# Tying interleaved VectorE work to the weight stream, and wider value matmuls, in a two-layer hybrid decoder trunk

## The chip, the cores and the metric

The kernel runs on one core of one Trainium2 chip. The metric is device time in microseconds (us) for one execution, and the figure for the kernel before is the median of three runs. A profile of one further execution gives the rows below. TensorE (PE) multiplies, VectorE (DVE) and ScalarE (ACT) do elementwise work and read PSUM, GpSimd (POOL) does elementwise work on SBUF, and SyncE (SP) issues all DMA loads and stores.

## The reference

Two layers work on x of shape 512 x 1024 (one batch). Per layer, in float32:

```
mod = silu(c) @ w_ada + b_ada                  # 6 x 1024: sh1, sc1, g1, sh2, sc2, g2
h = x * (1 + sc1) + sh1
p = h @ w_in                                   # q,k,v,g of retention; q,f,v,g of HGRN2; conv a,b; gates
u_a = retention(...); u_b = hgrn2(...); u_c = silu(LN(dwconv31(ca * sigmoid(cb))))
y = sum over 3 branches of sigmoid(gate_i) * (u_i @ w_branch[i])
x = LN(ALPHA * x + g1 * (y @ w_out)) * ln1_g + ln1_b
h = x * (1 + sc2) + sh2
f = (silu(a) * v) @ w_down,  a, v = split(dwconv3(h @ w_up))        # d_ff 2816
x = LN(ALPHA * x + g2 * f) * ln2_g + ln2_b
```

Retention and HGRN2 have four heads of 128 each, the convolution has 512 channels and 31 taps.

## The kernel before

**Layout.** Activations lie feature-major: a tile is 128 features by 512 tokens. Each float32 operand of a large matmul is kept as two float32r parts, a high part `hi` and the rest `lo`, and `mm3` issues three matmuls for a product (hi x hi, hi x lo, lo x hi; lines 249 to 251). Weights come in chunks of 128 x 1024 (512 KB). The function `w_plan` writes their order out by hand for each layer.

**Weight stream.** `prefetch` takes a chunk through three steps: a DMA into `raw` (line 215, 4 buffers of the tag "raw"), a copy on ScalarE to `hi` (line 216) and a subtraction on VectorE for `lo` (line 217; 4 buffers each). `chunk(kind, ahead)` makes sure that the wanted chunk and `ahead` further ones have been prefetched and hands out the first; the usual `ahead` is LA = 2. Most projections (`proj`) use one chunk for 24 matmuls of 512 columns.

**Stages of a layer.** An input projection for the convolution, then the mixing half in the order of MIX: values of HGRN2, HGRN2 heads 0 and 1, values of retention, HGRN2 head 2, retention 0, HGRN2 3, retention 1 to 3. Then come three branches in the order HGRN2, retention, convolution: for each pair of 128 output features two gate projections, one branch chunk, two products. A branch product is multiplied by the gate on VectorE (line 802), added to the sum on GpSimd (line 806), and after the last branch split into hi and lo (lines 229 and 231). Then the output projection with the first norm, the feed-forward half, and its norm.

**Interleaved work.** Work that doesn't follow the stream is written as generators. `heads` holds the recurrences of the heads, `fill` a queue of other work: rope tables, the 31 taps of the convolution in two pairs of tiles (60 instructions a pair, line 383), the norm of the convolution, conditioning columns, residuals. After every four contraction tiles the projections call `tick(us)`, which adds a credit of at most 3.0, advances up to three heads by a step each and then takes steps of the first fill entry while credit is left. Each step returns its cost in credit. Steps of heads are tied behind the last matmul with `tc.issue_after`; steps of `fill` are not. The tool that builds the program orders each engine's queue itself, by a simulated time at which an instruction becomes ready and by its place in the program; `issue_after(ins)` adds an edge to `ins` for instructions of its own engine, without a semaphore. `drain(fill)` at the end of the mixing half finishes what is left.

**Conditioning.** `ada_col(l, i)` loads one 128 x 1024 chunk of w_ada (line 191) into a buffer of the same tag "raw" as the weights, multiplies and sums it against silu(c) (line 195) and adds the bias (line 196). Layer 0's first 16 columns are done in the start stage, 24 in the mixing half (as `rest(aux)` behind the convolution's norm), 8 in the feed-forward half, and the next layer's first 16 in the down projection. `affine` then computes eight gains and eight shifts one column at a time (lines 661 and 662) and two scaled copies (lines 664 and 666).

**Values.** `proj_tok` computes values token-major: h is the stationary operand, the weight chunk moves. Two groups of 256 columns are computed with two chunks each, a chunk holding 4 contraction tiles x 256 columns.

Of the kernel before, what the change touches and what calls it, by code (L numbers as in the profile page):

```python
# [20 lines left out]
P = 128  # L21
# [8 lines left out]
NB = 47  # L30
NHL = 4
LA = 2
NRAW = 4
TK = 1.7
AUX = 99
# [18 lines left out]
def w_plan(l):  # L54
# [7 lines left out]
    def tok(seg):  # L62
        return [("tok", c, SEG[seg] + 256 * g) for g in range(2) for c in range(2)]
# [26 lines left out]
def trunk(ctx, tc, xT, cT, pos, ada, bada, wts, cols, lbl, rope_c, decay, hmask, outT):  # L90
# [73 lines left out]
    last = [None]  # L164

    def step(queue, g):
        try:
            if queue is heads:
                with tc.issue_after(last[0].ins):
                    return next(g)  # L170
            return next(g)
        except StopIteration:
            queue.remove(g)
            return 0.0
# [14 lines left out]
    def ada_col(l, i):  # L189
        raw = wp.tile([P, 1024], F32, tag="raw", name=nm("ar"), bufs=NRAW)  # L190
        nc.sync.dma_start(raw, ada[l, i])
        o = ADA[i]
        dst = modt[l][:, o:o + 1]
        yield 0.0
        stt(raw, raw, 1.0, cond, ALU.mult, ALU.mult, accum_out=dst)  # L195
        ts(dst, dst, bad[:, 48 * l + o:48 * l + o + 1], 1.0 if o // 8 in (1, 4) else 0.0, ALU.add, ALU.add)
        yield 1.3
# [5 lines left out]
    def prefetch(n=1):  # L203
        for _ in range(n):
# [8 lines left out]
            for o in range(0, 1024, n):  # L213
                s = slice(o, o + n)
                nc.sync.dma_start(raw[:, s], wts[l, i][:, s])
                act(hi[:, s], raw[:, s], AF.Copy)  # L216
                tt(lo[:, s], raw[:, s], hi.bitcast(F32)[:, s], ALU.subtract)  # L217
# [72 lines left out]
    def proj_tok(hs):  # L290
        for g in range(2):
            w = [chunk("tok", LA - 1), chunk("tok", LA - 1)]
            for tp in range(2):
                q = pm()
                for t2 in range(2):
                    tk = 2 * tp + t2
                    dst = q[:, 256 * t2:256 * (t2 + 1)]
                    for kt in range(KT):
                        mm3(dst, sl2(hs[kt], 128 * tk), sl2(w[kt // 4], 256 * (kt % 4), 256),
                            kt == 0, kt == KT - 1)  # L300
                    tick(1.5)
                yield g, tp, q
# [72 lines left out]
    def conv_taps(l, i0, us, out, aux):  # L375
# [5 lines left out]
        for d in range(1, CK):  # L381
# [4 lines left out]
            if d % AUX == 0 and aux:  # L386
                yield from aux.pop(0)

    def rest(aux):
        while aux:  # L390
            yield from aux.pop(0)
# [59 lines left out]
    def hgrn_head(l, h, q, f, ke, sg, v, out):  # L451
# [12 lines left out]
        while m <= 256:  # L464
# [44 lines left out]
            else:  # L509
                act(pf[:, 128:384], z[:, 0:256], AF.Copy)  # L510
                act(pf[:, 384:512], z[:, 256:384], AF.Copy)
                act(pg[:, 0:128], z[:, 384:512], AF.Copy)
            m, lev = 2 * m, lev + 1
            yield 1.2
# [143 lines left out]
    def affine(l, gname, bname, lm, sc, sh):  # L658
        for j in range(8):
            G, B = gbt[:, j:j + 1], gbt[:, 8 + j:9 + j]  # L660
            stt(G, col(l, gname, j), -0.5, mod(lm, sc, j), ALU.mult, ALU.mult)
            stt(B, col(l, bname, j), mod(lm, sc, j), mod(lm, sh, j), ALU.mult, ALU.add)
        o = CO[gname]
        ts(gbt[:, 16:24], colt[l][:, o:o + 8], -0.5 * ALPHA, None, ALU.mult)
        o = CO[bname]
        ts(gbt[:, 24:32], colt[l][:, o:o + 8], ALPHA, None, ALU.mult)
# [46 lines left out]
    for j in range(8):  # L713
        cs = [ada_col(0, 2 * j), ada_col(0, 2 * j + 1)]
        for g in cs:
            next(g)
        nc.sync.dma_start(X[j], xT[j])
        for g in cs:
            next(g)
# [8 lines left out]
    for l in range(L):  # L728
# [5 lines left out]
        aux = [ada_col(l, i) for i in range(16, 40)]  # L734
# [3 lines left out]
        for i in (0, 2):  # L738
# [5 lines left out]
            fill.append(conv_taps(l, i, us, acc, aux))  # L744
        fill.append(conv_norm(l, acc, u_c))
        fill.append(rest(aux))

        vg, vr = [big() for _ in range(4)], [big() for _ in range(4)]
        for what, h in MIX:
            if what == "g" and h < 0:  # L750
                for g, tp, q in proj_tok(hs):
                    for t2 in range(2):
                        act(vg[2 * tp + t2][:, 256 * g:256 * (g + 1)], q[:, 256 * t2:256 * (t2 + 1)], AF.Copy)
            elif h < 0:
                for g, tp, q in proj_tok(hs):
                    qv = q.rearrange("p (t h d) -> p t h d", h=2, d=128)
                    sm = bp.tile([P, 4], F32, tag="sm", name=nm("sm"), bufs=2)
                    nc.vector.tensor_reduce(sm, q.rearrange("p (a d) -> p a d", d=128),
                                            mybir.AxisListType.X, ALU.add)
                    for t2 in range(2):  # L760
                        stt(vr[2 * tp + t2][:, 256 * g:256 * (g + 1)].rearrange("p (h d) -> p h d", d=128),
                            sm[:, 2 * t2:2 * t2 + 2].unsqueeze(2).broadcast_to([P, 2, 128]), -1.0 / 128,
                            qv[:, t2], ALU.mult, ALU.add)
# [16 lines left out]
        for bi, b in enumerate(ORDER):  # L780
            us = (u_a, u_b, u_c)[b]
            for jp in range(4):
# [13 lines left out]
                for t in range(2):  # L796
# [6 lines left out]
                    if bi == 0:  # L803
                        ys[j] = sg[t]
                    else:
                        ptt(ys[j], ys[j], sg[t], ALU.add)  # L806
# [4 lines left out]
        affine(l, "ln1g", "ln1b", l, 4, 3)  # L811
# [28 lines left out]
        fill.extend(ada_col(l, i) for i in range(40, 48))  # L840
# [20 lines left out]
        if l == 0:  # L861
            fill.extend(ada_col(1, i) for i in range(16))
# [3 lines left out]
        for j in range(8):  # L866
            parts = HALVES if j == 7 else ((0, S),)
            if l == 0 and j == 7:
                drain(fill)
                affine(l, "ln2g", "ln2b", 1, 1, 0)  # L870
# [39 lines left out]
def _chunks(l, w_in, w_branch, w_out, w_up, w_down):  # L910
    out = np.empty((NW, 128, 1024), np.float32)
    down = w_down.reshape(FT, 128, 8, 128).transpose(2, 0, 1, 3).reshape(FT, 8, 128, 128)
    for i, p in enumerate(W_PLAN[l]):
# [10 lines left out]
        elif p[0] == "tok":  # L924
            out[i] = _ktile(w_in, 4 * p[1], 4, p[2], 256)
# [78 lines left out]
```

## Time and profile before

| | before |
|---|---|
| median of 3 runs | 1846.57 us (1845.42 to 1847.24) |
| the profiled execution | 1846.69 us |
| its span, first to last instruction | 1844.90 us |
| mean granted TensorE clock | 0.996 |
| PE busy | 1805.0 us, 98% |
| DVE busy | 1290.4 us, 70% |
| ACT busy | 751.4 us, 41% |
| POOL busy | 218.8 us, 12% |
| HBM read | 214.19 MB, 117 GB/s over the span |

Busy time is the union of an engine's instructions. Ends of matmuls are modelled and matmuls overlap, so a busy TensorE isn't one at its peak: the distance between the starts of matmuls says more than their durations. Times in the rows are us from the start of the span, durations in "mean" columns are ns. [...]

### The profile page before, as it was taken

What the parts mean: (1) busy time and instruction counts of PE and PEld (TensorE: products, weight loads), DVE (VectorE), ACT (ScalarE), POOL (GpSimd) and SP (SyncE); (2) the same over time, 40 slices, a digit from 0 to 9 for tenths busy, and PEclk for the clock granted to TensorE, in tenths of its full rate; (3) what the DMA queues carried; (4) which work ended last, traced back from release to release, by engine and by line L of the source; (5) the groups of instructions that cost most, each with busy time, mean ns of one, the idle gap of its engine ahead of it and who ended that gap; (6) DMA issues with size and microseconds to landing.
All of it is one profiled execution on the core that took longest, in us unless ns stands there. A gap on an engine that the chain in (4) does not pass through costs nothing.

```text
span 1844.9 us, 23510 instructions
## 1 busy us (share of the span) xinstructions
PE 1805.0 (98%) x9156; PEld 1520.0 (82%) x9156; DVE 1290.4 (70%) x2025; ACT 751.4 (41%) x1042; POOL 218.8 (12%) x187
## 2 busy tenths in 40 slices
PE   7999999999999999999999999999999999999997
PEld 5888877888788888888889987778787988888886
DVE  6995565978869756667489565993775896666344
ACT  3434344333337444432273344453523564444232
POOL 3111231042100000000000221320222000000001
PEclk9999999999999999999999999999999999999999
DMA  8512222226624422255223112222474244222221
GB/s 304 195 70 80 75 75 80 92 103 213 228 73 144 142 103 92 103 183 182 93 90 103 70 69 75 71 76 99 156 245 158 81 142 143 92 103 92 102 82 46
DMA packets 63614, 217.81 MB, mean 118 GB/s; under 512 B 7440, under 2 KB 9872, under 8 KB 63504
## 3 DMA queue, kind: packets, MB, share of 16 engines
q1 hardware_dynamic: 63504, 216.32, 34.2%
q8 instruction: 72, 1.18, 0.3%
q14 instruction: 38, 0.31, 0.1%
HBM read 214.19 MB, written 2.10 MB: 117 GB/s over the span
## 4 chain that ended last, share of the span: by engine, by line
PE 79%; DVE 11%; DMA 4%; ACT 2%; issue 2%; POOL 2%; SPq 0%; DVEq 0%; POOLq 0%; ACTq 0%
PE pm L249 24%; PE pm L251 24%; PE pm L250 24%; DMA ar<-ada 4%; DVE wl L217 2%; DVE ar L195 2%; PE ps L477 2%; DVE b L383 1%; POOL b L806 1%; ACT wh L216 1%; DVE x L655 1%; PE po L552 1%; PE ps L544 1%; DVE b L802 1%; PE ps L250 0%
## 5 line engine op out<-in xcount | busy, mean ns | idle before, releaser
L249 PE MATMUL pm<-h,wh 128*128 128x512 f32 (+1 forms) x1568 | 613.3, 391 | 13.3 <-ACT wh L216 11.6
L251 PE MATMUL pm<-h,wl 128*128 128x512 f32 (+1 forms) x1568 | 603.3, 385 | 0.2
L250 PE MATMUL pm<-h,wh 128*128 128x512 f32 (+1 forms) x1568 | 602.1, 384 | 0.0
L217 DVE TENSOR_TENSOR wl<-wr,wh 128x1024 fp32r<-128x1024 f32 (+1 forms) x301 | 376.8, 1254 | 251.6 <-ACT wh L216 250.5
L216 ACT ACTIVATE wh<-wr 128x1024 fp32r<-128x1024 f32 (+1 forms) x301 | 317.1, 1055 | 490.0 <-PE pm L250 385.2
L249 PEld LDWEIGHTS pm<-h,wh 128*128 128x128 f32 x1568 | 295.6, 188 | 72.0 <-ACT wh L216 11.6
L251 PEld LDWEIGHTS pm<-h,wl 128*128 128x128 f32 x1568 | 295.0, 188 | 61.3 <-DVE wl L217 3.4
L250 PEld LDWEIGHTS pm<-h,wh 128*128 128x128 f32 x1568 | 295.5, 188 | 58.8 <-issue 1.9
L249 PE MATMUL pm<-b,wh 128*128 128x512 f32 (+1 forms) x764 | 280.8, 368 | 6.1 <-ACT b L229 4.7
L250 PE MATMUL pm<-b,wh 128*128 128x512 f32 (+1 forms) x764 | 279.5, 366 | 0.4 <-DVE b L231 0.4
L251 PE MATMUL pm<-b,wl 128*128 128x512 f32 (+1 forms) x764 | 279.1, 365 | 0.0
L383 DVE SCALAR_TENSOR_TENSOR b<-b,cols,b 128x511 f32<-128x511 f32 (+14 forms) x240 | 171.9, 770 | 0.0
L249 PEld LDWEIGHTS pm<-b,wh 128*128 128x128 f32 x764 | 145.0, 190 | 30.5 <-ACT b L229 5.6
L250 PEld LDWEIGHTS pm<-b,wh 128*128 128x128 f32 x764 | 145.0, 190 | 24.5 <-DVE b L231 1.5
L195 DVE SCALAR_TENSOR_TENSOR ar<-ar,cond 128x1024 f32<-128x1024 f32 x96 | 123.5, 1293 | 58.9 <-DMA ar<-ada 58.8
L251 PEld LDWEIGHTS pm<-b,wl 128*128 128x128 f32 x764 | 144.9, 190 | 22.8
L229 ACT ACTIVATE b<-b 128x512 fp32r<-128x512 f32 x88 | 55.4, 630 | 230.7 <-DVE b L852 109.2
L231 DVE TENSOR_TENSOR b<-b,b 128x512 fp32r<-128x512 f32 x88 | 61.1, 694 | 51.9 <-ACT b L229 51.8
L490 POOL TENSOR_TENSOR b<-b,b 128x256 f32<-128x256 f32 x64 | 56.3, 879 | 324.9 <-PE ps L477 218.0
L806 POOL TENSOR_TENSOR b<-b,b 128x512 f32<-128x512 f32 x32 | 57.1, 1784 | 235.2 <-DVE b L802 222.8
L249 PE MATMUL pm<-wh,h 128*128 128x256 f32 x256 | 73.7, 289 | 0.0
L250 PE MATMUL pm<-wl,h 128*128 128x256 f32 x256 | 72.4, 283 | 0.6 <-DVE wl L217 0.6
(222 smaller groups left out, 1899.5 us busy)
## 6 DMA issues: line engine op xcount, KB each, us to landing
wr<-wts SPq DMA_DIRECT2D x299, 512.0 KB, 3.5
ar<-ada SPq DMA_DIRECT2D x96, 512.0 KB, 4.3
x<-xT SPq DMA_DIRECT2D x8, 256.0 KB, 5.8
b<-decay SPq DMA_DIRECT2D x8, 256.0 KB, 3.8
outT<-b SPq DMA_DIRECT2D x16, 128.0 KB, 1.8
b<-hmask SPq DMA_DIRECT2D x3, 256.0 KB, 5.9
cond<-cT SPq DMA_DIRECT2D x1, 512.0 KB, 4.7
wr<-wts SPq DMA_DIRECT2D x2, 256.0 KB, 6.7
```

Source lines behind the costliest of these rows:

```text
L195: stt(raw, raw, 1.0, cond, ALU.mult, ALU.mult, accum_out=dst)
L216: act(hi[:, s], raw[:, s], AF.Copy)
L217: tt(lo[:, s], raw[:, s], hi.bitcast(F32)[:, s], ALU.subtract)
L229: act(hi, src, AF.Copy)
L231: tt(lo, src, hi.bitcast(F32), ALU.subtract)
L249: mm(dst, a[0], b[0], start=first, stop=False)
L250: mm(dst, a[0], b[1], start=False, stop=False)
L251: last[0] = mm(dst, a[1], b[0], start=False, stop=end)
L383: stt(a[:, d:S], us[i][:, 0:S - d], col(l, "cw", 4 * (CK - 1 - d) + i0 + i), a[:, d:S], ALU.mult, ALU.add)
L477: mm(z[:, 64 * i:64 * (i + 1)], ke[:, sl], rhs, start=True, stop=True)
L490: ptt(kv[:, :, 0, :], kv[:, :, 0, :], fv[:, :, 1:2].broadcast_to([P, nb, m]), ALU.mult)
L806: ptt(ys[j], ys[j], sg[t], ALU.add)
```

## The change

- **Ties.** `step` puts every step, of heads and of fill, behind the last matmul and behind `wlast[1]`, the VectorE subtraction of the weight chunk prefetched last.
- **Conditioning.** `ada_cols` handles a list of columns: it issues the load of the next column before it sums the current one, has three buffers of its own, ties its loads behind the last weight load, and adds biases for eight columns in one instruction. It goes into `fill` as an ordinary entry, and `affine` behind it, now eight columns at a time.
- **Values.** `proj_tok` computes 512 columns per matmul from four chunks of 2 contraction tiles x 512 columns, for two token tiles at a time, in two passes.
- **Due times.** A step of a HGRN2 head returns 1.0, 0.6 or 0.3 instead of 1.2.
- **Branch sums.** The addition of the branches moves from GpSimd to VectorE.
- **Buffers.** 48 instead of 47 of the 128 x 512 buffers; a scratch area for DMA descriptors is made smaller.

```diff
-NB = 47
+NB = 48
+NADA = 3
     def tok(seg):
-        return [("tok", c, SEG[seg] + 256 * g) for g in range(2) for c in range(2)]
+        return [("tok", c, SEG[seg]) for c in range(4)]
...
+    wlast = [None, None]
     def step(queue, g):
         try:
-            if queue is heads:
-                with tc.issue_after(last[0].ins):
-                    return next(g)
-            return next(g)
+            with tc.issue_after(last[0].ins), tc.issue_after(wlast[1].ins):
+                return next(g)
...
-    def ada_col(l, i):
-        raw = wp.tile([P, 1024], F32, tag="raw", name=nm("ar"), bufs=NRAW)
+    def ada_load(l, i, tag="ada"):
+        raw = wp.tile([P, 1024], F32, tag=tag, name=nm("ar"), bufs=NADA if tag == "ada" else NRAW)
         nc.sync.dma_start(raw, ada[l, i])
-        o = ADA[i]
-        dst = modt[l][:, o:o + 1]
-        yield 0.0
-        stt(raw, raw, 1.0, cond, ALU.mult, ALU.mult, accum_out=dst)
-        ts(dst, dst, bad[:, 48 * l + o:48 * l + o + 1], 1.0 if o // 8 in (1, 4) else 0.0, ALU.add, ALU.add)
-        yield 1.3
+        return raw
+
+    def ada_sum(l, i, raw):
+        stt(raw, raw, 1.0, cond, ALU.mult, ALU.mult, accum_out=modt[l][:, ADA[i]:ADA[i] + 1])
+
+    def ada_bias(l, s, o, n):
+
+        dst = modt[l][:, 8 * s + o:8 * s + o + n]
+        b = 48 * l + 8 * s + o
+        stt(dst, dst, 1.0 if s in (1, 4) else 0.0, bad[:, b:b + n], ALU.add, ALU.add)
+
+    def ada_cols(l, idx):
+
+
+        raw = None
+        for i, j in zip(idx, [*idx[1:], None]):
+            with tc.issue_after(wlast[0].ins):
+                if raw is None:
+                    raw = ada_load(l, i)
+                nxt = None if j is None else ada_load(l, j)
+            ada_sum(l, i, raw)
+            raw = nxt
+            yield 1.3
+        for s in sorted({ADA[i] // 8 for i in idx}):
+            ada_bias(l, s, 0, 8)
+        yield 0.3
...
-                nc.sync.dma_start(raw[:, s], wts[l, i][:, s])
+                wlast[0] = nc.sync.dma_start(raw[:, s], wts[l, i][:, s])
                 act(hi[:, s], raw[:, s], AF.Copy)
-                tt(lo[:, s], raw[:, s], hi.bitcast(F32)[:, s], ALU.subtract)
+                wlast[1] = tt(lo[:, s], raw[:, s], hi.bitcast(F32)[:, s], ALU.subtract)
...
     def proj_tok(hs):
-        for g in range(2):
-            w = [chunk("tok", LA - 1), chunk("tok", LA - 1)]
-            for tp in range(2):
-                q = pm()
+
+
+        w = []
+        for tp in range(2):
+            qs = [pm(), pm()]
+            for c in range(4):
+                if tp == 0:
+                    w.append(chunk("tok", LA if c < 2 else 3 - c))
                 for t2 in range(2):
-                    tk = 2 * tp + t2
-                    dst = q[:, 256 * t2:256 * (t2 + 1)]
-                    for kt in range(KT):
-                        mm3(dst, sl2(hs[kt], 128 * tk), sl2(w[kt // 4], 256 * (kt % 4), 256),
+                    for k in range(2):
+                        kt = 2 * c + k
+                        mm3(qs[t2], sl2(hs[kt], 128 * (2 * tp + t2)), sl2(w[c], 512 * k, 512),
                             kt == 0, kt == KT - 1)
-                    tick(1.5)
-                yield g, tp, q
+                    if t2:
+                        tick(1.5)
+            for t2 in range(2):
+                yield 2 * tp + t2, qs[t2]
...
+            yield 1.0 if m < 32 else 0.6 if m < 128 else 0.3
             m, lev = 2 * m, lev + 1
-            yield 1.2
...
     def affine(l, gname, bname, lm, sc, sh):
-        for j in range(8):
-            G, B = gbt[:, j:j + 1], gbt[:, 8 + j:9 + j]
-            stt(G, col(l, gname, j), -0.5, mod(lm, sc, j), ALU.mult, ALU.mult)
-            stt(B, col(l, bname, j), mod(lm, sc, j), mod(lm, sh, j), ALU.mult, ALU.add)
-        o = CO[gname]
-        ts(gbt[:, 16:24], colt[l][:, o:o + 8], -0.5 * ALPHA, None, ALU.mult)
-        o = CO[bname]
-        ts(gbt[:, 24:32], colt[l][:, o:o + 8], ALPHA, None, ALU.mult)
+        g, b = (colt[l][:, CO[n]:CO[n] + 8] for n in (gname, bname))
+        sc, sh = (modt[lm][:, 8 * k:8 * k + 8] for k in (sc, sh))
+        stt(gbt[:, 0:8], g, -0.5, sc, ALU.mult, ALU.mult)
+        tt(gbt[:, 8:16], b, sc, ALU.mult)
+        tt(gbt[:, 8:16], gbt[:, 8:16], sh, ALU.add)
+        ts(gbt[:, 16:24], g, -0.5 * ALPHA, None, ALU.mult)
+        ts(gbt[:, 24:32], b, ALPHA, None, ALU.mult)
+        yield 1.0
...
         fill.append(conv_norm(l, acc, u_c))
-        fill.append(rest(aux))
+        fill.append(ada_cols(l, range(16, 40)))
+        fill.append(affine(l, "ln1g", "ln1b", l, 4, 3))
...
-                        ptt(ys[j], ys[j], sg[t], ALU.add)
+                        tt(ys[j], ys[j], sg[t], ALU.add)
...
         drain(fill)
-        affine(l, "ln1g", "ln1b", l, 4, 3)
...
-        fill.extend(ada_col(l, i) for i in range(40, 48))
+        fill.append(ada_cols(l, range(40, 48)))
...
-            fill.extend(ada_col(1, i) for i in range(16))
+            fill.append(ada_cols(1, range(16)))
```

The copies of the values to SBUF follow the new shape: 512 columns at a time on ScalarE for HGRN2, and for retention a reduction and one subtraction of the mean over 512 columns per token tile on VectorE.

## Rows read from the trace of the kernel before

**Rows 1.** The page's busy table: busy us, share of the span, instructions.
```profile
PE 1805.0 (98%) x9156; PEld 1520.0 (82%) x9156; DVE 1290.4 (70%) x2025; ACT 751.4 (41%) x1042; POOL 218.8 (12%) x187
```

**Rows 2.** Groups by line and shape: TensorE's matmuls, then value weight loads.
```profile
L249 PE MATMUL pm<-h,wh 128*128 128x512 f32 x1472 | 586.5, 398 | 13.3 <-ACT wh L216 11.6 <-ACT b L787 1.7
...
L249 PE MATMUL pm<-b,wh 128*128 128x512 f32 x580 | 228.0, 393 | 6.1 <-ACT b L229 4.7 <-ACT b L787 1.4
...
L249 PE MATMUL pm<-wh,h 128*128 128x256 f32 x256 | 73.7, 289 | 0.0
...
L249 PEld LDWEIGHTS pm<-wh,h 128*128 128x128 f32 x256 | 49.1, 192 | 0.3
```

**Rows 3.** Timeline of TensorE: start us, duration us; ends of two stretches.
```profile
60.27 0.28 PE L249 MATMUL pm<-wh,h 128*128 128x256 f32 x1
...
82.71 0.28 PE L251 MATMUL pm<-wh,h 128*128 128x256 f32 x1
...
340.04 0.39 PE L249 MATMUL pm<-h,wh 128*128 128x512 f32 x1
...
344.57 0.39 PE L251 MATMUL pm<-h,wl 128*128 128x512 f32 x1
```

**Rows 4.** Busy us (count) by stretches: PE, PEld, DVE, ACT, POOL; clock, DMA, GB/s.
```profile
450.00:498.00 48.00, 47.74 (x210) 39.12 (x210) 38.90 (x68) 11.96 (x16) 10.38 (x6) 1.00 0.66 226
498.00:517.00 19.00, 12.70 (x40) 8.85 (x39) 11.37 (x18) 6.87 (x9) 3.43 (x3) 0.82 0.57 189
...
1070.00:1140.00 70.00, 70.00 (x364) 57.72 (x363) 39.56 (x56) 28.22 (x45) 15.60 (x16) 1.00 0.25 87
1140.00:1235.00 95.00, 90.60 (x429) 69.97 (x428) 93.38 (x143) 45.93 (x64) 21.13 (x17) 1.00 0.21 70
...
1308.00:1386.00 78.00, 75.21 (x330) 61.42 (x329) 60.30 (x107) 30.85 (x39) 17.39 (x10) 1.00 0.66 216
1386.00:1426.00 40.00, 39.84 (x176) 32.68 (x175) 23.31 (x35) 14.91 (x20) 10.26 (x6) 1.00 0.48 158
```

**Rows 5.** VectorE's waits: us in total, times, longest us.
```profile
DVE wl L217 <- ACT wh L216: 250.5, 127, 5.3
DVE ar L195 <- DMA ar<-ada: 58.8, 38, 6.1
```

**Rows 6.** Timelines of ScalarE, VectorE, GpSimd and TensorE, branches of layer 0.
```profile
399.17 1.06 ACT L216 ACTIVATE wh<-wr 128x1024 fp32r<-128x1024 f32 x1 [3.38 <-PE pm L250]
...
394.83 1.23 DVE L217 TENSOR_TENSOR wl<-wr,wh 128x1024 fp32r<-128x1024 f32 x1 [3.32 <-ACT wh L216]
...
400.27 2.34 DVE L217 TENSOR_TENSOR wl<-wr,wh 128x1024 fp32r<-128x1024 f32 x1
...
400.24 1.29 POOL L806 TENSOR_TENSOR b<-b,b 128x512 f32<-128x512 f32 x1 [1.49 <-DVE b L802]
...
506.52 0.50 PE L249 MATMUL pm<-b,wh 128*128 128x512 f32 x1 [1.93 <-ACT b L229]
```

**Rows 7.** Timeline of VectorE, first projection of layer 0.
```profile
52.33 0.58 DVE L664 TENSOR_SCALAR gbt<-cols 128x8 f32<-128x8 f32 x1
```

**Rows 8.** Groups by line and shape: VectorE.
```profile
L802 DVE TENSOR_TENSOR b<-pm,b 128x512 f32<-128x512 f32 x48 | 32.9, 686 | 11.3 <-PE pm L251 11.3
...
L196 DVE TENSOR_SCALAR mod<-mod,bad 128x1 f32<-128x1 f32 x96 | 19.2, 208 | 0.8
...
L662 DVE SCALAR_TENSOR_TENSOR gbt<-cols,mod 128x1 f32<-128x1 f32 x24 | 6.2, 261 | 0.5
```

**Rows 9.** VectorE busy by stretches, taps (line 383) alone; clock, DMA, GB/s.
```profile
318.00:400.00 82.00, 43.30 (x60) 1.00 0.27 97
...
1140.00:1235.00 95.00, 40.13 (x53) 1.00 0.21 70
```

**Rows 10.** Timeline of VectorE: the convolution's norm in layer 0, first and last.
```profile
402.58 2.48 DVE L408 SCALAR_TENSOR_TENSOR b<-po,b 128x512 f32<-128x512 f32 x4
...
435.49 0.68 DVE L231 TENSOR_TENSOR b<-b,b 128x512 fp32r<-128x512 f32 x1
```

## What the change does to the time, predicted

> **What bounds the kernel now.** I read the page's busy table first: TensorE is busy for 1805 of 1844.9 us [rows 1]. The kernel is a stream of matmuls, so the change can win in two ways only: fewer or cheaper matmul slots, or fewer holes in the stream. Second, how dear is a slot? The mean duration of a 512-wide matmul is 398 ns and of a 256-wide one 289 ns [rows 2], but these overlap: one line alone has 586.5 us of the 1472 first ones and 228.0 us of 580 others, it is one of three with as many, and 3 x 814.5 us is more than the span. So I took the distance between starts in a quiet stretch: from 60.27 to 82.71 us there are 187 steps of 256-wide value matmuls, 22.44 / 187 = 0.120 us each; from 340.04 to 344.57 us 20 steps of 512-wide ones, 4.53 / 20 = 0.227 us each [rows 3]. Third, where are the holes? The table by stretches shows them [rows 4]. [...] 1140 to 1235 us (retention heads of layer 1) lacks 4.4 us, with VectorE 98% busy; 1308 to 1386 us (layer 1's convolution norm and conditioning columns) lacks 2.8 us. [...] Last, the waits of VectorE: 250.5 us for the weights' high half, which come just in time and cost TensorE nothing, and 58.8 us for conditioning columns still in flight [rows 5].
>
> **Wide value matmuls.** Each of the four value projections (two per layer) has 2 x 4 x 8 x 3 = 192 matmuls 256 wide, 768 in all (each of three lines has 256, [rows 2]). After it has 96 matmuls 512 wide. The saving is 192 x 0.120 - 96 x 0.227 = 23.04 - 21.76 = 1.28 us, 5.1 us for four. [...] The other end is a stall: the four chunks are now consumed in one pass, 12 matmuls or 2.7 us each, and the fourth takes the buffer of the chunk before. That is freed when the projection begins, ACT takes 1.06 us and VectorE 1.23 us [rows 6], so it is ready at 2.3 us and needed at 8.2 us. The next chunk's buffer comes free 2.7 us into the second pass, 8.2 us ahead of need. The value projection's own copies sit between them in the program, but this scheduler lets work that is ready pass: the scaling of a norm gain, written behind the whole mixing half, ran at 52.3 us, during the first projection [rows 7]. I take no stall; if one conversion were late each time, 4 x 2.3 = 9.2 us would turn the gain into 4 us lost.
>
> **The sums of the branches move from GpSimd to VectorE.** 32 adds leave a path on which GpSimd took 1.29 us and more [rows 6]; at 0.69 us, as the multiply of the same shape [rows 8], they put 22 us on VectorE. They also give some back: the weight subtraction that ran beside a GpSimd add took 2.34 us, the one before it 1.23 us [rows 6]. A branch output is split at least 0.6 us earlier.
>
> **Conditioning columns and affine.** 96 bias instructions become 26 (16 in the start stage, then 3 + 1 per layer and 2 for the next layer's start): 70 x 0.208 = 14.6 us off VectorE. Affine goes from 54 to 15 instructions: 39 x 0.26 = 10 us at most [rows 8]. So VectorE's sum is 22 - 14.6 - 10 = -2.6 us: nothing. What matters is the 58.8 us of waits: each sum now follows a load issued one step earlier, out of three buffers that weights don't share. SyncE has these loads behind the last weight load, and a load waits only for the sum three columns back, so the weight loads queued behind it are not held. In the start stage loads, order and shared buffers stay; I cost it at nothing (one small VectorE instruction replaces another).
>
> **The ties and the due times.** Each step of heads and fill now stands behind the last matmul and, on VectorE, behind the last weight chunk's subtraction. That chunk is two ahead. Its buffer comes free when the chunk two before the current one is finished, so it is done 2.3 us into the previous chunk, which lasts 24 x 0.227 = 5.4 us: 3.1 us before the step. Queued behind it are the heads' instructions, for which TensorE waits; cost nothing as long as VectorE lags by less than that. The fill's place in the order does change. A recurrence head now charges 0.6 + 5 x 1.0 + 2 x 0.6 + 2 x 0.3 = 7.4 instead of 0.6 + 9 x 1.2 = 11.4, 16 less per layer. Credits up to the point where the third branch needs the convolution's output: 24 (value) + 81.6 (heads) + 73.6 (two branches) + 4.4 = 183.6. Charged before: heads 81.3, rope 5.3, taps 72, norm 17, together 175.6, so 8 to spare; after, 24. With 22.8 more credits to the end, the 24 columns and affine (32.5) fit with 14 to spare; before, they did not. So columns stop crowding the end of layer 0.
>
> **The holes.** End of layer 0: TensorE waited for the split of a branch output [rows 6] because VectorE was full of columns and their waits (38.9 of the 48 us before, [rows 4]). Idle 6.3 us, and 0.18 x 19 = 3.4 us for the clock. Layer 1, whose columns were done earlier, loses 0.2 us there, so I take 9.5. At 1308 to 1386 us, 2.8 less 0.3: 2.5. The heads' hole of layer 1 (4.4) is open both ways. It came where the second pair's taps fell among the heads: 53 of them at 1140 to 1235 us, while layer 0 ran its 60 later, at 318 to 400 us [rows 9]. Earlier fill spreads them over the lull at 1070 to 1140 us (VectorE 57%), but in layer 0 it moves them into the heads. Best: 4.4 gained; worst: layer 0 gets layer 1's hole and layer 1's doubles, 8.8 lost. Between these I take zero.
>
> **Sum.** The profiled execution took 1846.69 us, 1.79 of it outside the span; the median of the runs is 1846.57, so no correction. 1846.7 - 5.1 - 9.5 - 2.5 = 1829.6, say 1830 us. Its own range: 1825 to 1838, by the ends of the heads' hole.
>
> **Rivals.**
> - Only the matmuls gain: each hole closed opens elsewhere. For it: VectorE's work is unchanged and taps cluster. Against it: layer 1 shows the end without a hole. 1846.7 - 5.1 = 1841.6.
> - The heads become VectorE-bound in both layers. The stretch of 98% loses 4.4 us per 95. Over 1070 to 1235 us and its twin in layer 0 that is 2 x 7.6 = 15.3, half as dense again, as more fill is pulled in, 23, against 4.4 now: up to +18.5, which eats the 17. About 1847. For it: heads wait for VectorE at every level. Against it: VectorE is free for 30 us in the lull [rows 4].
> - Slower: the tied taps, which could run ahead before, are not done when the third branch asks. It decides once VectorE lags by the 24 credits. TensorE then waits for the whole norm, 402.6 to 436.2 us before [rows 10], 33.6 us, less two projections of 5.4: 23 us a layer. One layer: 1846.7 - 5.1 + 23 = 1865. For it: tied work cannot fill the early gaps. Against it: the spare is three times that of before.
> - The slot price is the duration: 768 x 0.289 - 384 x 0.398 = 69 us less, which with the holes gives 1766. Against it: the sum of durations exceeds the span. [...]
>
> **How the numbers follow.** Chances: the forecast 0.58, matmuls alone 0.17, heads bound 0.13, late norm 0.08, slot price 0.04. With the heads' hole gone the forecast is 1825; 1820 leaves 5 us below that for the small holes that I did not itemise. 1845 holds the forecast, the second case and part of the third, some 0.82. A difference under 0.2% (3.7 us) can't be told from none. Faster: 0.58 + 0.04 + 0.14 of the second case (it lies 5.1 us off) + 0.02 of the third, 0.78. Within: 0.03 + 0.08 = 0.11. Slower: 0.08 + 0.03 = 0.11.
>
> **What would show it.** Right: value matmuls 512 wide, 0.227 us apart; no wait of VectorE for a conditioning column in the branches; the last column long before the output projection, whose first matmuls don't wait, with the clock at its full level; busy VectorE where the lull was. Wrong: new waits of TensorE for the weights' low half in the value projections; waits for head tiles growing in 100 to 320 us and its twin in layer 1; a stall before the third branch. The sum fails most easily in the heads, whose term I could only bound.

## The result, and the profile after

The changed kernel takes 1825.67 us (median of four runs, 1824.18 to 1826.89). The kernel before, on the same chip, took 1846.9 us; the ratio is 0.9885 with a 95% interval of 0.9868 to 0.9902, a gain of 21 us. The profiled execution took 1824.18 us with a span of 1822.4 us, so 22.5 us of span went. The page's busy table, against [rows 1]:

```profile
PE 1793.5 (98%) x8772; PEld 1498.1 (82%) x8772; DVE 1279.5 (70%) x1940; ACT 753.5 (41%) x1035; POOL 160.4 (9%) x155
```

384 matmuls are gone, VectorE does 11 us less in spite of 32 more additions, and GpSimd lost 58 us. The groups by line and shape, against [rows 2] and [rows 8], show the wide value matmuls, the branch sums in their new place, and the biases eight at a time (`mm3` now stands at lines 268 to 270):

```profile
L268 PE MATMUL pm<-wh,h 128*128 128x512 f32 x128 | 51.1, 403 | 0.0
...
L819 DVE TENSOR_TENSOR b<-b,b 128x512 f32<-128x512 f32 x32 | 22.1, 690 | 0.7
...
L200 DVE SCALAR_TENSOR_TENSOR mod<-mod,bad 128x8 f32<-128x8 f32 x10 | 1.3, 161 | 0.0
```

The timeline of TensorE (start, duration) gives the price of a wide value matmul. These are the first matmul of layer 1's HGRN2 values and the first one behind them, 96 steps apart: 21.76 / 96 = 0.227 us, the price that the prediction used.

```profile
956.44 0.39 PE L268 MATMUL pm<-wh,h 128*128 128x512 f32 x1
...
978.20 0.39 PE L268 MATMUL pm<-h,wh 128*128 128x512 f32 x1
```

The table by stretches, with the stretches of [rows 4] moved to where the same work lies now (end of layer 0's branches, its output projection, the lull and the retention heads of layer 1, and layer 1's columns, which now run early in its branches):

```profile
444.50:492.50 48.00, 48.00 (x213) 39.75 (x213) 25.20 (x39) 16.27 (x21) 0.00 (x0) 1.00 0.37 133
492.50:511.50 19.00, 19.00 (x86) 15.72 (x85) 10.22 (x14) 5.82 (x7) 0.00 (x0) 1.00 0.31 109
...
1052.00:1122.00 70.00, 66.76 (x347) 54.35 (x346) 53.10 (x82) 24.44 (x40) 13.91 (x14) 1.00 0.21 72
1122.00:1217.00 95.00, 94.11 (x453) 74.66 (x453) 75.71 (x114) 51.05 (x70) 22.79 (x20) 1.00 0.22 75
1266.00:1344.00 78.00, 78.00 (x346) 64.56 (x344) 63.08 (x98) 28.06 (x35) 0.00 (x0) 1.00 0.68 236
```

The hole at the end of layer 0's mixing half and the one in layer 1's branches are closed, at a granted clock of 1.00 (a share of full speed), and the retention heads of layer 1 are no longer short of VectorE (75.7 of 95 us against 93.4). In their place the lull has a hole of 3.2 us that was not there before. The waits (us, times, longest) name it, and show that VectorE waits far less for conditioning columns, 14.4 us against 58.8 [rows 5]; of the 14.4, 5.6 lie in the start stage.

```profile
PE pm L268 <- ACT b L461: 3.0, 1, 3.0
...
DVE ar L194 <- DMA ar<-ada: 14.4, 16, 5.4
```

The timeline of the last column of layer 0 and of a last branch product: multiply, add, high part (lines 815, 819, 248) now follow one another on VectorE and ScalarE. The last column, which stood just ahead of the last products in the kernel before:

```profile
499.81 1.21 DVE L195 SCALAR_TENSOR_TENSOR ar<-ar,cond 128x1024 f32<-128x1024 f32 x1
```

now starts more than 40 us ahead of them:

```profile
450.64 1.22 DVE L194 SCALAR_TENSOR_TENSOR ar<-ar,cond 128x1024 f32<-128x1024 f32 x1
...
491.90 0.69 DVE L815 TENSOR_TENSOR b<-pm,b 128x512 f32<-128x512 f32 x1 [0.58 <-PE pm L270]
492.62 0.69 DVE L819 TENSOR_TENSOR b<-b,b 128x512 f32<-128x512 f32 x1
...
493.35 0.63 ACT L248 ACTIVATE b<-b 128x512 fp32r<-128x512 f32 x1 [2.80 <-DVE b L819]
```

The new hole, on the same three engines:

```profile
1063.74 2.53 DVE L404 TENSOR_SCALAR b<-b,cols 128x512 f32<-128x512 f32 x2
1066.19 5.36 DVE L407 SCALAR_TENSOR_TENSOR b<-b,cols,b 128x511 f32<-128x511 f32 x8
1071.47 0.68 DVE L333 SCALAR_TENSOR_TENSOR b<-po,b 128x512 f32<-128x512 f32 x1
...
1075.73 0.68 DVE L454 TENSOR_TENSOR b<-b,b 128x512 f32<-128x512 f32 x1
...
1076.44 0.63 ACT L248 ACTIVATE b<-b 128x512 fp32r<-128x512 f32 x1 [4.49 <-DVE b L454]
1077.09 1.28 ACT L460 ACT_TABLE_LOAD   x1
...
1078.88 0.59 ACT L461 ACTIVATE b<-pm 128x512 f32<-128x512 f32 x1
...
1079.52 0.50 PE L268 MATMUL pm<-h,wh 128*128 128x512 f32 x1 [3.00 <-ACT b L461]
```

Ten taps run as one block of 7.9 us in front of the output of a HGRN2 head (L333 to L454). ScalarE's split of that output (L248) waits for it, the gates of the next head (L460, L461) stand behind the split in ScalarE's queue, and only they free the PSUM tile that TensorE needs.

**Stages.** To see where each kernel gains I added up, in each profile, the distance from the first matmul of a stage to the first matmul of the next (the matmuls of `mm3` come in the same order in all of them; with narrow values only their count differs). "Heads" runs from HGRN2 head 2 to the end of the first branch (branch 0), "end" is the third branch and the output projection.

| us | before | after |
|---|---|---|
| four value projections | 117.0 | 112.2 |
| layer 0: heads | 210.6 | 211.0 |
| layer 0: branch 1 | 66.3 | 66.3 |
| layer 0: end | 123.0 | 112.0 |
| layer 1: heads | 216.0 | 215.4 |
| layer 1: branches 1 and 2 | 135.2 | 130.6 |

These make 20.6 of the 22.5 us; 1.4 more lie ahead of the values (start and first projection, which spread by 2.7 us among the profiles of this study), the rest in layer 1's output projection. All other stages are equal within 0.1 us, but for the start.

### The profile page after: what moved, and what is told of

The parts are those of the page before. It is cut to its first block, busy times and chain, and to the rows that moved or that the text cites. A ratio compares the mean times of both kernels' runs of the same rounds, so it can differ in the third digit from the quotient of the medians.

```text
span 1822.4 us, 22665 instructions
## 1 busy us (share of the span) xinstructions
PE 1793.5 (98%) x8772; PEld 1498.1 (82%) x8772; DVE 1279.5 (70%) x1940; ACT 753.5 (41%) x1035; POOL 160.4 (9%) x155
## 4 chain that ended last, share of the span: by engine, by line
PE 91%; DVE 5%; ACT 2%; DMA 1%; issue 1%; POOL 0%; SPq 0%; DVEq 0%; ACTq 0%; POOLq 0%
PE pm L268 28%; PE pm L270 28%; PE pm L269 28%; PE ps L495 2%; PE ps L562 1%; DVE wl L236 1%; PE po L570 1%; DVE ar L194 1%; DMA wr<-wts 1%; DVE x L673 1%; DMA ar<-ada 1%; ACT wh L235 1%; PE ps L489 0%; PE ps L478 0%; ACT n L696 0%
## 5 line engine op out<-in xcount | busy, mean ns | idle before, releaser
L236 DVE TENSOR_TENSOR wl<-wr,wh 128x1024 fp32r<-128x1024 f32 (+1 forms) x301 | 374.6, 1248 | 304.9 <-ACT wh L235 304.4
L407 DVE SCALAR_TENSOR_TENSOR b<-b,cols,b 128x511 f32<-128x511 f32 (+14 forms) x240 | 168.6, 751 | 0.0
L194 DVE SCALAR_TENSOR_TENSOR ar<-ar,cond 128x1024 f32<-128x1024 f32 x96 | 116.1, 1219 | 14.7 <-DMA ar<-ada 14.4
L248 ACT ACTIVATE b<-b 128x512 fp32r<-128x512 f32 x88 | 55.4, 629 | 170.5 <-DVE b L864 97.0
L859 DVE SCALAR_TENSOR_TENSOR b<-pm,cols,b 128x510 f32<-128x510 f32 x84 | 62.5, 748 | 2.2
L857 ACT ACTIVATE b<-pm,cols 128x512 f32<-128x512 f32 x84 | 63.5, 761 | 0.0
L858 DVE SCALAR_TENSOR_TENSOR b<-pm,cols,b 128x511 f32<-128x511 f32 x84 | 62.1, 743 | 0.0
```

What stands on the lines that cost most here:

```text
L194: stt(raw, raw, 1.0, cond, ALU.mult, ALU.mult, accum_out=modt[l][:, ADA[i]:ADA[i] + 1])
L236: wlast[1] = tt(lo[:, s], raw[:, s], hi.bitcast(F32)[:, s], ALU.subtract)
L407: stt(a[:, d:S], us[i][:, 0:S - d], col(l, "cw", 4 * (CK - 1 - d) + i0 + i), a[:, d:S], ALU.mult, ALU.add)
L857: act(a, q, AF.Identity, bias=col(l, "fb", i), scale=col(l, "fw", 88 + i))
L858: stt(a[:, 1:S], q[:, 0:S - 1], col(l, "fw", 44 + i), a[:, 1:S], ALU.mult, ALU.add)
L859: stt(a[:, 2:S], q[:, 0:S - 2], col(l, "fw", i), a[:, 2:S], ALU.mult, ALU.add)
```

## Experiments

Twelve kernels: parts of the change alone in the kernel before, parts taken out of the changed kernel, and sums of parts. The medians and the stages, as in the table above:

| us | median (range) | ratio to before, interval | values | L0 heads | L0 br. 1 | L0 end | L1 heads | L1 br. 1+2 |
|---|---|---|---|---|---|---|---|---|
| b_wide | 1840.13 (1837.89 to 1840.69) | 0.9960 [0.9948, 0.9973] | 112.0 | 210.6 | 66.3 | 121.5 | 215.8 | 134.7 |
| b_dveadd | 1832.03 (1831.74 to 1833.43) | 0.9920 [0.9907, 0.9934] | 117.0 | 210.6 | 66.3 | 112.0 | 215.8 | 132.0 |
| b_cols | 1842.12 (1839.77 to 1843.04) | 0.9975 [0.9966, 0.9984] | 117.0 | 210.6 | 70.4 | 112.5 | 215.8 | 137.1 |
| b_ties | 1832.35 (1830.96 to 1833.59) | 0.9920 [0.9907, 0.9934] | 117.0 | 211.0 | 66.3 | 112.5 | 215.5 | 130.6 |
| b_tiesonly | 1838.29 (1836.19 to 1839.08) | 0.9953 [0.9940, 0.9965] | 117.0 | 211.2 | 66.3 | 122.3 | 211.3 | 132.5 |
| b_wideadd | 1827.02 (1826.16 to 1827.56) | 0.9894 [0.9879, 0.9909] | 112.0 | 210.6 | 66.3 | 112.0 | 216.0 | 132.0 |
| b_wideaddties | 1821.85 (1821.67 to 1822.25) | 0.9866 [0.9852, 0.9879] | 112.0 | 211.2 | 66.3 | 112.0 | 211.4 | 131.6 |
| a_untied | 1839.42 (1835.45 to 1840.89) | 0.9959 [0.9944, 0.9974] | 112.0 | 216.6 | 71.0 | 112.0 | 220.6 | 130.6 |
| a_oldcols | 1827.20 (1826.16 to 1827.45) | 0.9895 [0.9879, 0.9912] | 112.0 | 211.0 | 66.3 | 112.0 | 217.8 | 130.6 |
| a_pool | 1827.74 (1826.30 to 1829.16) | 0.9899 [0.9885, 0.9914] | 112.0 | 211.0 | 66.3 | 112.5 | 215.5 | 130.6 |
| a_due12 | 1822.28 (1821.96 to 1822.69) | 0.9870 [0.9855, 0.9885] | 112.0 | 211.2 | 66.3 | 112.0 | 211.3 | 131.6 |
| a_dueflat | 1820.44 (1819.70 to 1821.43) | 0.9858 [0.9845, 0.9872] | 112.0 | 210.4 | 66.3 | 112.0 | 211.6 | 130.6 |

### Taken out of the changed kernel

**a_oldcols**: conditioning columns as before (shared buffers, load and sum without a column in between, one bias each), in their new place in `fill`.

```diff
     def ada_cols(l, idx):
-        raw = None
-        for i, j in zip(idx, [*idx[1:], None]):
-            with tc.issue_after(wlast[0].ins):
...
-            ada_bias(l, s, 0, 8)
+        for i in idx:
+            raw = ada_load(l, i, "raw")
+            yield 0.0
+            ada_sum(l, i, raw)
+            ada_bias(l, ADA[i] // 8, ADA[i] % 8, 1)
+            yield 1.3
```

> The changed kernel with the conditioning columns loaded as before: each into a buffer shared with the weights, the load issued in the same step as its sum, one bias instruction per column. Theory (the hole at the end of layer 0 came from columns that were still being done when the output projection was due; the new due times alone now bring them early enough): VectorE waits for columns again, 40 to 60 us, but earlier, and the output projection of layer 0 stays at 47 to 50 us; total 1826 to 1831 us. Rival (loading ahead into own buffers is what closed it): the output projection goes back to 53 to 56 us, total 1833 to 1837.

It took 1827.2 us, 1.5 more than the changed kernel, and the two ranges overlap; its profile has 2.4 us more in layer 1's heads. The 40 to 60 us of waits that were expected did not come: its VectorE waits 9.8 us for columns, less than the 14.4 above. Loading ahead and own buffers are worth little here, and they are not what removed the waits.

**a_pool**: the sums of the branches back on GpSimd.

```diff
-                        tt(ys[j], ys[j], sg[t], ALU.add)
+                        ptt(ys[j], ys[j], sg[t], ALU.add)
```

> The changed kernel with the branch sums on GpSimd as before. Theory (columns were the cause, the adder's engine not): output projection of layer 0 stays within 1 us of 46.8, total 1825 to 1828 us. Rival (the slow GpSimd add held the last split): the output projection of layer 0 takes 50 us or more and the second and third branches of layer 1 lose 2 us and more; total 1831 to 1836.

1827.74 us, 2 more than after, with overlapping ranges; each output projection took 0.5 us longer, and the hole at the end of layer 0 did not come back.

**a_untied**: `step` as in the kernel before: fill untied, heads behind the last matmul alone.

```diff
-            with tc.issue_after(last[0].ins), tc.issue_after(wlast[1].ins):
-                return next(g)
+            if queue is heads:
+                with tc.issue_after(last[0].ins):
+                    return next(g)
+            return next(g)
```

> The changed kernel with the ties as before: steps of heads behind the last matmul, steps of fill free. Theory (ties cost and gain little, since the weight chunk they stand behind is done a chunk earlier): 1823 to 1829 us, TensorE's waits for the weights' low half within 1 us of the changed kernel's. Rival (the ties are what removed the holes): 1835 us or more, with holes in the heads of layer 1 of 4 us and more.

1839.42 us: without the ties 14 of the 21 us are lost, in the heads of both layers (+5.7 and +5.1) and in layer 0's branch 1 (+4.7). The timeline of branch 1 in that kernel (columns L196, norm of the convolution L441 and L442, gate of the branch L802):

```profile
399.21 1.21 DVE L196 SCALAR_TENSOR_TENSOR ar<-ar,cond 128x1024 f32<-128x1024 f32 x1
...
400.36 2.49 DVE L441 TENSOR_TENSOR b<-b,b 128x512 f32<-128x512 f32 x4
...
401.07 1.52 ACT L442 ACTIVATE b<-b,cols 128x512 f32<-128x512 f32 x2 [0.67 <-DVE b L441]
...
403.02 1.51 ACT L442 ACTIVATE b<-b,cols 128x512 f32<-128x512 f32 x2
404.55 1.28 ACT L802 ACT_TABLE_LOAD   x1
405.84 0.60 ACT L802 ACTIVATE b<-pm 128x512 f32<-128x512 f32 x1
```

The gate that TensorE waits for (2.8 us in the waits of this kernel) stands in ScalarE's queue behind work of the norm, which came late from a VectorE that ran eight columns between 380 and 400 us. So the ties, which I had costed at nothing, cannot be taken out of the changed kernel without most of its gain. That is not yet what they give on their own; b_wideadd, below, has nearly the whole gain without them.

**a_due12**: the due times of the kernel before, a level of a HGRN2 head returns 1.2.

```diff
-            yield 1.0 if m < 32 else 0.6 if m < 128 else 0.3
             m, lev = 2 * m, lev + 1
+            yield 1.2
```

> The changed kernel with the old due times: each level of a recurrence head charges 1.2. Theory (16 credits fewer for the fill per layer push the columns back towards the end of layer 0): columns run some 25 us later, the output projection of layer 0 takes 49 to 53 us, total 1828 to 1834. Rival (the loads ahead are enough whatever the due times): output projection 47 us, total within 1 us of 1825.7.

1822.28 us: 3.4 faster than the changed kernel, and the slowest run of the one is faster than the fastest of the other, though the intervals of the two ratios overlap. Both expectations were wrong: the new due times cost time. Layer 1's heads take 211.3 us instead of 215.4, and the wait of 3.0 us is gone.

### Parts alone, in the kernel before

**b_wide**: the wide value matmuls alone (the chunks of `w_plan`, `proj_tok`, the copies).

```diff
-        return [("tok", c, SEG[seg] + 256 * g) for g in range(2) for c in range(2)]
+        return [("tok", c, SEG[seg]) for c in range(4)]
```

> The kernel before with the wide value matmuls alone. Theory (the price of a matmul is the distance of starts): each value projection 1.0 to 1.3 us shorter, 4.8 to 5.1 us in all, total 1841 to 1843 us, with the hole at the end of layer 0 still there. Rival (price by durations): 60 us and more, total under 1790. [...]

1840.13 us. The value projections give 5.0 us, as expected. The profile has a further 1.5 and 0.5 us in the ends of the mixing halves, which the expectation did not have, and takes 1.3 us more ahead of the values, within the spread of that part.

**b_dveadd**: the branch sums on VectorE alone, the diff of a_pool the other way round.

> The kernel before with the branch sums on VectorE alone. Theory: the adds put 22 us on VectorE and give back the time in which weight subtractions stood beside GpSimd adds; the end of layer 0 keeps most of its hole since VectorE is still full of columns: output projection 51 to 56 us, total 1841 to 1848. Rival (the GpSimd add was the cause): output projection of layer 0 47 to 49 us, total 1834 to 1839.

1832.03 us, below both expectations. This one word of the code gives 14.7 us and closes the end of layer 0 by itself. Neither the loads ahead nor the ties are needed for that. Its VectorE still waits for columns nearly as long as before (in layer 0's branches and output projection 12.1 us against 16.4):

```profile
DVE ar L195 <- DMA ar<-ada: 50.6, 37, 5.5
```

**b_cols**: the conditioning and affine of the change alone (own buffers, load ahead, loads tied on SyncE's queue, biases by eight, its place in `fill`).

> The kernel before with the new conditioning alone: loads one step ahead in own buffers, biases and affine eight columns at a time. Theory (columns were in the way at the end of layer 0, by their waits and by their place in the queue): most of that hole goes, the output projection of layer 0 takes 47 to 50 us instead of 55.6, total 1835 to 1841. Rival (only the due times or the adder matter): hole stays within 1 us, total 1845 to 1848.

1842.12 us, 1 more than expected: the end of layer 0 is closed as well, but branch 1 takes 4.1 us longer in layer 0 and 3.7 in layer 1. The longest waits of TensorE in this kernel, behind the start, are for the sums of the convolution's norm (L257, L258):

```profile
PE po L264 <- ACT b L257: 3.8, 2, 2.5
PE po L266 <- POOL b L258: 2.2, 3, 0.8
```

**b_ties**: the ties and the new due times, nothing else.

```diff
+            with tc.issue_after(last[0].ins), tc.issue_after(wlast[1].ins):
+                return next(g)
...
+            yield 1.0 if m < 32 else 0.6 if m < 128 else 0.3
             m, lev = 2 * m, lev + 1
-            yield 1.2
```

> The kernel before with the ties and the new due times alone. Theory (due times bring the columns forward, ties cost nothing): output projection of layer 0 shorter by 4 to 9 us, total 1835 to 1843. Rival (ties hold the fill back in early gaps): the hole grows or the third branch waits for the convolution, total over 1850.

1832.35 us, less than expected, and this too closes the end of layer 0 alone. It has the new stall of layer 1 as well (TensorE waits 3.0 us for the same gate), so that stall doesn't come from the wide values or the new columns.

**b_tiesonly**: the ties without the due times, the first half of that diff.

> The kernel before with the ties alone: steps of heads and fill behind the last matmul and the last weight subtraction; a level of a HGRN2 head still returns 1.2. The kernel before with ties and new due times took 1832.4 us, and the new due times cost 3.4 us in the changed kernel. Theory: the ties alone close the end of layer 0 (branch 2 and output projection 112 to 113 us, against 123.0 before), and without the new due times the 3.2 us stall in layer 1 at 1076 us is not there (g2 to r1 of layer 1 91 to 92 us): 1827 to 1831 us. Rival: the earlier credit of the new due times is what brings the columns out of the end; then that end stays over 116 us and the time is 1836 to 1842.

1838.29 us; the rival was right on the end of layer 0, which stays at 122.3 us, while the heads of layer 1 are 4.7 us shorter. The timeline at its end of layer 0: the last matmul of a branch product, then column, weight subtraction, multiply, add, split, and TensorE behind it:

```profile
494.84 0.39 PE L250 MATMUL pm<-b,wl 128*128 128x512 f32 x1
...
499.45 1.22 DVE L194 SCALAR_TENSOR_TENSOR ar<-ar,cond 128x1024 f32<-128x1024 f32 x1
...
501.43 1.23 DVE L216 TENSOR_TENSOR wl<-wr,wh 128x1024 fp32r<-128x1024 f32 x1 [0.25 <-ACT wh L215]
502.57 0.68 DVE L801 TENSOR_TENSOR b<-pm,b 128x512 f32<-128x512 f32 x1
...
503.40 1.26 POOL L805 TENSOR_TENSOR b<-b,b 128x512 f32<-128x512 f32 x1 [9.20 <-DVE b L801]
...
504.69 0.63 ACT L228 ACTIVATE b<-b 128x512 fp32r<-128x512 f32 x1 [2.81 <-POOL b L805]
...
505.38 0.67 PE L248 MATMUL pm<-b,wh 128*128 128x512 f32 x1 [3.35 <-ACT b L228]
```

And VectorE's wait for columns in the same kernel:

```profile
DVE ar L194 <- DMA ar<-ada: 7.2, 5, 5.4
```

So the ties alone take away the waits for columns, 7.2 us against 58.8 [rows 5] (between 450 and 505 us there is none), and the hole stays. It does not come from those waits. The product whose last matmul stands in the first line is multiplied only at 502.57 us, more than 7 us later; in between VectorE runs three columns (495.51, 498.31 and 499.45 us), with their small instructions, and two weight subtractions, and its longest wait is 0.25 us. So what makes the hole is the columns themselves, at that place. In all the runs the hole goes with it: the last column starts at 499.81 us before, 499.45 here and 497.83 in b_wide, within 1.7 us of the first matmul of the output projection, and these three have the hole. In b_dveadd it starts at 489.98, in b_cols at 485.43, in a_due12 at 488.62, in b_ties at 461.44, and these have none; in every run without the hole it lies 5.8 us or more ahead of that matmul. In b_dveadd the last products then wait for TensorE alone:

```profile
489.98 1.22 DVE L195 SCALAR_TENSOR_TENSOR ar<-ar,cond 128x1024 f32<-128x1024 f32 x1
...
495.38 0.69 DVE L802 TENSOR_TENSOR b<-pm,b 128x512 f32<-128x512 f32 x1 [0.58 <-PE pm L251]
496.11 0.69 DVE L806 TENSOR_TENSOR b<-b,b 128x512 f32<-128x512 f32 x1
...
496.83 0.63 ACT L229 ACTIVATE b<-b 128x512 fp32r<-128x512 f32 x1 [2.80 <-DVE b L806]
```

### Sums of parts

**b_wideadd** and **b_wideaddties**: the kernel before with wide values and branch sums on VectorE, and the same with the ties; due times and columns as before.

> The kernel before with wide value matmuls and the branch sums on VectorE, nothing else. Theory: the two gains add, 1832.0 less 4.8 for the values: 1826 to 1829, with the end of layer 0 at 111 to 113 us. Rival: the wide values shift the order so that something opens elsewhere, as it did when each part was made alone: 1831 or more.

> The kernel before with wide value matmuls, branch sums on VectorE and the ties; due times and conditioning columns as before. Theory: this is all that the change is worth, and without the new due times a little more: 1820 to 1824. Rival: the reworked columns are needed once the rest is tied (their own buffers, 1.5 us in the changed kernel) and the time is 1825 or more.

1827.02 and 1821.85 us, both as the first theory had it. Two plain edits give nearly all of the gain; with the ties the median is 3.8 us below that of the whole change, and its slowest run is faster than the fastest of the change, though the intervals of the two ratios overlap. Next to b_wideaddties, a_due12 has the reworked columns besides, and takes the same time (1822.28), stage by stage.

**a_dueflat**: the changed kernel with one price for each of a head's nine levels, 6.84 a head in all, against 6.8.

```diff
-            yield 1.0 if m < 32 else 0.6 if m < 128 else 0.3
+            yield 0.76
```

> The changed kernel with one price of 0.76 for each of the nine levels of a HGRN2 head, 6.84 a head, against 5 x 1.0 + 2 x 0.6 + 2 x 0.3 = 6.8: the same credit, spread evenly. Theory: the stall in layer 1 comes from the low price of the last levels, which lets a burst of taps in just ahead of the head's output; spread evenly there is no stall of 3 us, g2 to r1 of layer 1 take 91 to 92.5 us, and the time is 1821 to 1824. Rival: what counts is the sum of the credits, which brings the second pair of taps forward to the place where the heads change; then the stage stays at 94 to 95.5 and the time at 1825 to 1827.

1820.44 us, the lowest median of all, 0.6 below the range of the theory, and the stall is gone as the theory had it. The last column of layer 0 still comes early (451.23 us), and the block of taps in front of the head's output is gone; the split of that output waits for nothing:

```profile
1066.49 1.40 DVE L407 SCALAR_TENSOR_TENSOR b<-b,cols,b 128x507 f32<-128x507 f32 x2
1068.41 0.69 DVE L333 SCALAR_TENSOR_TENSOR b<-po,b 128x512 f32<-128x512 f32 x1 [0.51 <-ACT b L332]
...
1070.58 0.69 DVE L454 TENSOR_TENSOR b<-b,b 128x512 f32<-128x512 f32 x1
...
1071.31 0.63 ACT L248 ACTIVATE b<-b 128x512 fp32r<-128x512 f32 x1
```

## Why the prediction was right, and where it was not

The median is 4.3 us below the forecast of 1830, and 0.7 above the lower end of its own range of 1825 to 1838. The places were right and each closed hole gave more than forecast; that the heads came out at their zero is luck, as below. The terms:

- **Wide value matmuls: -5.1 predicted, -4.8 measured.** The price of 0.227 us held; no stall came with the new order of the chunks. The forecast was 1.28 us for each of the four, and they gave 1.7, 0.9, 1.3 and 0.9 in the order of time: only layer 1's HGRN2 values, value matmuls alone and without a wait in both kernels, are the plain case. The first had a wait of 0.6 us for a low half before, and in retention's two, where head matmuls run between, part of the saving did not come; why stays open. b_wide, with 5.0 us in these stages, bears the rows out.
- **End of layer 0: -9.5 predicted, -10.95 measured. The place was right, half of the cause was wrong.** The term was read from 498 to 517 us and from the same place one layer on, 1386 to 1426 us [rows 4]. Columns in front of the last products make the hole; VectorE's waits for the columns' loads do not (b_tiesonly has lost the waits and kept the hole, b_dveadd kept most of the waits and lost the hole). It isn't one part's merit either: branch sums on VectorE, columns reworked, or ties with new due times close it one by one, so their single gains (14.7, 4.6, 14.4) don't add. Why the builder puts the last column 10 us earlier when only the sums move engine stays open.
- **The credits: right.** The working said that lower prices of the heads' levels bring the columns out of the end. b_tiesonly and b_ties differ in this alone, and the last column moves from 499.45 to 461.44 us.
- **Branches of layer 1: -2.5 predicted, -4.65 measured.** The mechanism was right, the term too small: I took the idle time of one stretch of 78 us, while by the distances of first matmuls branch 1 had lost 2.8 us and the third branch behind it 1.8.
- **The heads: 0 predicted, -0.2 measured, and wrong inside.** That the sum came out is luck. In layer 1 two effects cancel. The ties alone shorten these stages from 216.0 to 211.3 us, about the best end of the bounds that I gave (4.4); the new due times give 4.1 of it back (211.3 in a_due12, 215.4 after). I had looked at the due times only as a sum of credits. a_dueflat has the same sum without the stall, so it is the low price of a head's last levels: credit is left for a burst of taps exactly where the head's output is due.
- **The ties: costed at nothing, and that failed.** "Cost nothing as long as VectorE lags by less than that" asked only what a tie can delay. What it keeps away is the other side: work that may run as soon as it is ready runs in front of work that TensorE needs soon. With the reworked columns and new due times it is worth 14 us (a_untied), with the old ones 5.2 (b_wideadd to b_wideaddties). a_untied differs from b_wideadd in the columns and the due times and is 12 us slower. b_cols, with untied new columns and old due times, loses 4.1 us in layer 0's branch 1 where a_untied loses 4.7, so the columns are part of it; the share of the due times stays open.
- **Columns one load ahead, biases and affine by eight: the counted terms about right, and worth nothing next to the other parts.** The terms that I counted (sums, biases, affine) come to about 3.5 us less by the groups, against 2.6. VectorE lost 10.9 us of busy time [rows 1], since I had given no size to what other instructions get back. By the groups, the 96 sums of columns went from 123.5 to 116.1 us, the 240 taps from 171.9 to 168.6 and the 301 weight subtractions from 376.8 to 374.6, 13 us at the same counts and shapes; groups overlap in time and others grew, so they do not add up to the engine's total. TensorE sees none of the reworked columns: a_due12 and b_wideaddties differ in them alone and take the same time. The sign "no wait of VectorE for a conditioning column in the branches" came only in part: 2.5 us of such waits are left in layer 0's mixing half and 6.3 in layer 1's, against 16.4 and 12.7.

Of the rivals, holes that open elsewhere did come true in part: one of 3.2 us in the lull, and two in b_cols. The late norm never showed in the changed kernel; its relative, the norm's work in the way of branch 1, showed only without the ties.

## What to carry to other kernels

When an engine's queue is ordered by readiness, ask of each piece of filler not only when it must be done but what it may overtake: here a tie that orders filler behind the stream was worth 5 us in one kernel and 14 in another, and I had costed it at nothing. If one hole goes away with each of several edits, its gain belongs to none of them, and only sums of parts show which edits are needed; here two plain edits and the ties do at least as well as the whole change. Prices that steer filler want to be checked at the places where they are low, since that is where the filler bunches.

## What the runs showed of the hardware

The first finding is on the granted clock. In b_tiesonly the stretches around the stall of 3.4 us show it at 1.00 up to the end of the stall, then at 0.52 and 0.50 for some 10 us more, with a second, shorter wait of 2.3 us among them; in the last of these rows TensorE is busy throughout but does 9 matmuls in 3.4 us, where 0.227 us each make 15. The end of layer 0 takes 10.3 us longer than in b_dveadd; these waits are 5.6 us of it.

```profile
502.00:505.40 3.40, 0.06 (x2) 0.03 (x1) 1.30 (x3) 0.71 (x2) 1.26 (x1) 1.00 0.93 331
505.40:508.80 3.40, 1.86 (x3) 0.66 (x3) 2.38 (x3) 0.87 (x1) 2.01 (x1) 0.52 0.23 88
508.80:512.20 3.40, 2.58 (x5) 1.78 (x6) 1.29 (x2) 1.66 (x2) 0.10 (x1) 0.50 0.46 151
512.20:515.60 3.40, 3.40 (x9) 2.64 (x8) 1.29 (x2) 0.03 (x1) 0.00 (x0) 0.50 0.30 99
```

In the changed kernel the stretch with the stall of 3.0 us and the one behind it both show 1.00:

```profile
1076.00:1079.50 3.50, 0.52 (x3) 0.10 (x1) 3.50 (x6) 3.01 (x5) 0.00 (x0) 1.00 0.25 87
1079.50:1083.00 3.50, 3.48 (x22) 3.10 (x22) 2.27 (x6) 3.46 (x5) 0.00 (x0) 1.00 0.16 66
```

In a_untied the wait of 2.8 us in branch 1, shorter than this one, was followed by a stretch at a mean granted clock of 0.68, with 11 matmuls in 3.4 us of unbroken work.

```profile
406.50:409.90 3.40, 3.40 (x11) 2.71 (x12) 3.40 (x8) 2.93 (x5) 0.00 (x0) 0.68 0.75 249
```

What sets the two cases apart, no run here shows.

The second finding is on GpSimd's sums. In b_tiesonly a sum that began 0.1 us after a weight subtraction on VectorE took 2.25 us, while the subtraction kept its 1.22; the one at 503.40 us above, with VectorE free, took 1.26. In the kernel before, a weight subtraction that began 0.03 us after a sum took 2.34 us, the one ahead of it in the rows 1.23, and that sum took 1.29 [rows 6].

```profile
491.85 1.22 DVE L216 TENSOR_TENSOR wl<-wr,wh 128x1024 fp32r<-128x1024 f32 x1
...
491.95 2.25 POOL L805 TENSOR_TENSOR b<-b,b 128x512 f32<-128x512 f32 x1 [2.13 <-DVE mod L195]
```

What made the one of each pair longer, no run here shows.
